# A hybrid encoder block whose input projection begins with a block of 512 tokens, taken slice by slice of the features

## The chip, the cores and the metric

The kernel runs on one core of a Trainium2 chip. A core has a matrix engine (TensorE, PE in the profile, with PEld for its weight loads), VectorE (DVE), ScalarE (ACT), GpSimd (POOL) and SyncE (SP), which here issues the transfers. The metric is the device time of one execution in microseconds (us); the median of several executions is compared.

## The reference

One layer of an encoder over 2048 tokens of 1024 features, all in float32. What matters here is its head:

```python
xn = rms_norm(h, ln_mix_g[l])          # x / sqrt(mean(x*x) + eps) * g
proj = xn @ w_in[l]                    # 1024 x 2512 columns
y_a = mlstm_group(proj[..., OFF_Q:OFF_K], proj[..., OFF_K:OFF_V], proj[..., OFF_V:OFF_O],
                  proj[..., OFF_O:OFF_G], proj[..., OFF_G:OFF_CQ] + b_gates[l], ...)
y_b = mla_group(proj[..., OFF_CQ:OFF_CKV], proj[..., OFF_CKV:OFF_KR], proj[..., OFF_KR:IN_COLS], ...)
h = h + concatenate([y_a, y_b]) @ w_out[l]
```

The last 464 columns of the projection, called the rest here, are 16 gates, a query latent of 256, a key/value latent of 128 and 64 columns that are rotated by position. Behind the mixer come a gated feed-forward with a convolution, a gated per-layer embedding and a final norm.

## The kernel before

Every float32 operand of a projection is split in a high part, rounded to the type of TensorE's fast path, and a low part, the remainder. A product is three matmuls: low x high, high x low, high x high. `split` makes the high part of x with a ScalarE copy and the low part with a VectorE subtraction; `split_g` does the same for weights and multiplies them by the norm's gain (`gcol`) on the way. The factor 1/rms of a token is applied behind the matmul, from `rcol`, one column for each tile of 128 tokens.

`in_proj` (line 176) runs four stages over the 16 token tiles (`st`): the rest columns, the v columns, the o columns, and the q and k columns.

- *The rest stage.* `load_w` fetches the 464 columns of weights in pairs of feature slices of 128 and splits them into eight tiles. `load_x` fetches one token tile of x, all 1024 features of 128 tokens, 512 KB. In step `st` of the loop tile `st + 1` is loaded, tile `st` is split, the norm of tile `st - 1` is summed (`ssq_x`), the projection of tile `st - 2` is done (`rest`, which calls `nat`: 24 matmuls of 464 columns into one PSUM bank) and a tile two steps older is transposed (`turn_rest`). The first tile comes in two halves between the first weight slices (`first`).
- *The norm.* `ssq_x` squares x on ScalarE, adds on VectorE, sums over the partitions with small matmuls against `ones` into a tile of the pool `ml`, which has a single buffer, and takes the power -1/2 on GpSimd. VectorE reads the sum out of PSUM in line 239 (214 in the changed kernel).
- *What `rest` does behind its matmuls.* It writes the gates to `gt`, scales the other columns out of PSUM (`rs`), norms the two latents, rotates 64 columns and leaves the result in `nn`; `turn_rest` transposes that on TensorE and stores it.
- *The v and o stages.* Each tile is 24 matmuls of 512 columns; the output goes through a buffer taken from the rotation `trot` (tags t0 to t3 in turn) and is stored. Behind the first tiles of the v stage stand the last `turn_rest` calls, and from tile 2 on one step per tile of `gates`, a generator that prepares the gate values.
- *The q and k stage.* Its convolution (`taps`, `silu`) takes its tiles from the same `trot`. The last three, for `j` = 7, are made in `tail`, beside the first tiles of attention: there `other`, the mLSTM's generator, runs its first seven steps, one buffer of `trot` is skipped, three `taps` follow, and some steps later three Silu, pinned to their order. The mLSTM's `load_v` puts chunk c of v into the tag t0 or t1 (`c % 2`), from chunk 15 downwards, and its running state starts in t2.
- *PSUM.* The pool `sc` has four banks (`bank`), `tr` two (`tbank`), `pv` one, `ml` one.

The order of the instructions on each engine comes from a planner, except inside `manual_schedule`, where the listed engines keep the order of the code. It is fixed when the program is built. SP issues nearly all transfers, in one queue; a transfer that waits for a buffer holds up those behind it. Buffers are named by tags: a new tile with a tag waits until the readers of the old one are done. The tags w9 to w12 (`rrot`) hold in turn the raw weights and the token tiles of x; w13 holds the squares.

Of the kernel before, what the change touches and what calls it, by code (L numbers as in the profile page):

```python
# [19 lines left out]
P = 128  # L20
S = 2048
D = 1024
KT = D // P
NT = S // P
# [5 lines left out]
OFF_R = 2048  # L30
NREST = W_IN_COLS - OFF_R
# [2 lines left out]
PLE = 256  # L34
EPS = 1e-6
SB = 512
LAG_T, LAG_X, LAG_R = 1, 2, 2
SIDE = 668
KSCALE = 128.0 ** -0.5
ASCALE = 192.0 ** -0.5  # L40
# [12 lines left out]
def _rot(kind, idx):  # L53
    idx = list(idx)
    i = 0
    while True:
        yield f"{kind}{idx[i % len(idx)]}"
        i += 1


class Block:
# [114 lines left out]
    def in_proj(self):  # L176
        nc, d = self.nc, self.d
        xh = [[self.at(f"x{4 * c + 2 * f}", [P, 4, 512], F32R, f"xh{c}{f}") for f in range(2)] for c in range(4)]
        xl = [[self.at(f"x{4 * c + 2 * f + 1}", [P, 4, 512], F32R, f"xl{c}{f}") for f in range(2)] for c in range(4)]
        wrot, rrot, trot, srot = _rot("w", (*range(9), 13)), _rot("w", range(9, 13)), _rot("t", range(4)), _rot("s", range(3))  # L180
        w_in = d["w_in"][0].rearrange("(a b p) c -> a p b c", b=2, p=P)

        def load_w(c0, n, before=None):

            out, raws = [], []

            def load(k2, parts=1):
                raw = self.at(next(rrot), [P, 2, 512], name="wraw")
                for i in range(parts):
                    bs = slice(2 * i // parts, 2 * (i + 1) // parts)  # L190
                    nc.sync.dma_start(raw[:, bs, :n], w_in[k2, :, bs, c0:c0 + n])
                raws.append(raw)
                return raw

            if before:
                load(0, 2)
                before(0)
                load(1, 2)
                before(1)
                load(2)  # L200
                load(3)
            for k2 in range(KT // 2):
                if k2 == len(raws):
                    load(k2)
                raw = raws[k2]
                for b in range(2):
                    w = self.at(next(wrot), [P, 2, 512], F32R, "wsp")
                    self.split_g(raw[:, b, :n], gcol[:, 2 * k2 + b:2 * k2 + b + 1], w[:, 0, :n], w[:, 1, :n])
                    out.append(w)
            return out  # L210

        def nat(st, ws, n):
            ps = self.bank()
            c, o = st // 4, (st % 4) * P
            for kt in range(KT):
                f, k = divmod(kt, 4)
                self.mm3(ps[:, :n], xh[c][f][:, k, o:o + P], xl[c][f][:, k, o:o + P],
                         ws[kt][:, 0, :n], ws[kt][:, 1, :n], kt == 0, kt == KT - 1)
            return ps

        def load_x(st):

            t = self.at(next(rrot) if st else "u2", [P, KT, P], name="x_t")
            if st:
                nc.sync.dma_start(t, d["x_turned"][:, :, st * P:(st + 1) * P])
            return t

        def ssq_x(st, x_t):

            sq = self.at("w13", [P, KT, P], name="x_sq")  # L230
            nc.scalar.activation(sq, x_t, AF.Square)
# [3 lines left out]
            ps = self.pml.tile([P, 4], F32, name="ssp", tag="ml")  # L235
            for i in range(2):
                nc.tensor.matmul(ps, ss[:, i], ones, start=i == 0, stop=i == 1)
            t = self.stat(1, "rsm")
            nc.vector.tensor_scalar(t, ps[:, 0:1], 1.0 / D, EPS, op0=ALU.mult, op1=ALU.add)
            nc.gpsimd.tensor_tensor(rcol[:, st:st + 1], t, self.nhalf[:, :1], op=ALU.pow)  # L240
# [7 lines left out]
        def rest(st):  # L248
            ps = nat(st, ws, NREST)
# [28 lines left out]
        def turn_rest(st, nn):  # L278
            pt = self.ppv.tile([P, 4, P], F32, name="rtp", tag="pv")
            for j in range(4):  # L280
                nc.tensor.transpose(pt[:, j, :], nn[:, j * P:(j + 1) * P], self.ident)
# [5 lines left out]
        nc.sync.dma_start(gcol, d["g_turned"])  # L287
        rcol = self.cst.tile([P, NT], F32, name="rcol")
        ones = self.cst.tile([P, 4], F32, name="ones")
        nc.vector.memset(ones, 1.0)  # L290
        nq, xq = {}, {}

        xq[0] = load_x(0)

        def first(f):

            fs = slice(4 * f, 4 * f + 4)
            if f < 2:
                nc.sync.dma_start(xq[0][:, fs], d["x_turned"][:, fs, 0:P])
# [1744 lines left out]
```

## Time and profile before

| what | us |
|---|---|
| median of 3 executions | 2901.97 |
| lowest, highest | 2898.76, 2902.77 |
| the profiled execution's own time | 2898.51 |
| its span, first to last instruction | 2896.7 |
| TensorE busy | 2854.7 |
| VectorE, ScalarE busy | 2029.8, 1524.2 |

The page gives for each engine the busy time, then groups of instructions by line. In a row of the timeline the first number is the start in the span, the second the length, then engine, line, operation, output and inputs, and how often; in brackets stands the idle time before it and what ended it. SPq rows are transfers being issued. In a table of windows each row is a stretch of time with the busy time of PE, PEld, DVE, ACT and POOL, the granted TensorE clock (1.00 is full), the DMA share and GB/s. TensorE is the engine that is nearly always busy, so what counts is where it is idle or slow.

### The profile page before, as it was taken

To read this page: it belongs to the slowest core of one execution; us is meant where nothing else is said; L and a number is where in the kernel's file an instruction comes from. 1 tells how busy PE (TensorE), PEld (TensorE's weight loads), DVE (VectorE), ACT (ScalarE), POOL (GpSimd) and SP (SyncE) were. 2 spreads that over 40 slices of the span, in tenths; PEclk is the share of its full clock that TensorE was granted. 3 is DMA by queue.
4 is the path that set the end of the run, shared out by engine and by line. 5 is a ranking of instruction groups with operands and counts; after the bars stand their busy time and mean duration, and the time that the engine had idled before them with its cause. 6 is when DMAs were issued, how large, how long until landed. Compare 5 with 4: busy or idle time off the path is not lost.

```text
span 2896.7 us, 41145 instructions
## 1 busy us (share of the span) xinstructions
PE 2854.7 (99%) x14622; PEld 2416.9 (83%) x14622; DVE 2029.8 (70%) x3758; ACT 1524.2 (53%) x3014; POOL 157.1 (5%) x295
## 2 busy tenths in 40 slices
PE   8999999999999999999999999999999999999998
PEld 7888888888888889888788888888888788888787
DVE  7521555777777777776777877867777867676787
ACT  7311544556666666665755555655556333254665
POOL 3100000000000010001000000000000000011111
PEclk9999999999999999999999999999999999999999
DMA  6512545653332333378844554657766757576764
GB/s 189 132 59 77 162 125 163 218 162 117 105 111 98 97 104 113 126 244 267 276 145 165 193 174 147 220 176 235 234 230 210 241 187 249 166 265 205 263 217 163
DMA packets 408318, 509.00 MB, mean 176 GB/s; under 512 B 34080, under 2 KB 271664, under 8 KB 408112
## 3 DMA queue, kind: packets, MB, share of 16 engines
q1 hardware_dynamic: 408112, 506.37, 53.8%
q8 instruction: 115, 1.88, 0.3%
q14 instruction: 91, 0.75, 0.1%
HBM read 324.16 MB, written 182.12 MB: 175 GB/s over the span
## 4 chain that ended last, share of the span: by engine, by line
PE 58%; DMA 3%; DVE 3%; issue 2%; ACT 2%; POOL 0%; POOLq 0%; SPq 0%; ACTq 0%; DVEq 0%
PE fy L1434 21%; PE fz L1434 14%; PE fx L1434 14%; PE ppv L133 2%; PE fs L133 1%; PE tb L977 1%; DMA opr<-t_d 1%; DMA h_d<-xt 1%; PE bk L914 1%; PE bk L916 1%; PE bk L915 1%; PE bk L917 1%; PE bk L918 1%; DMA opr<-tw_d 1%; DVE op L123 1%
## 5 line engine op out<-in xcount | busy, mean ns | idle before, releaser
L1434 PE MATMUL fz<-op,fw 128*128 128x512 f32 x1968 | 478.8, 391 | 4.5 <-ACT fw L120 4.0
L1434 PE MATMUL fx<-op,fw 128*128 128x512 f32 x1968 | 476.4, 390 | 0.0
L1434 PE MATMUL fy<-op,fw 128*128 128x512 f32 x1968 | 475.3, 390 | 0.6 <-ACT fy L1546 0.6
L1434 PEld LDWEIGHTS fz<-op,fw 128*128 128x128 f32 x1968 | 368.4, 188 | 82.4 <-ACT fw L120 5.4
L1434 PEld LDWEIGHTS fy<-op,fw 128*128 128x128 f32 x1968 | 368.6, 188 | 77.3 <-ACT fy L1546 1.0
L1434 PEld LDWEIGHTS fx<-op,fw 128*128 128x128 f32 x1968 | 368.2, 188 | 76.1 <-ACT fy L1546 0.2
L1434 PE MATMUL fy<-op,fwd 128*128 128x512 f32 (+1 forms) x984 | 238.2, 390 | 1.9 <-DVE uv L1419 1.5
L120 ACT CAST pt<-tb 128x512 fp32r<-128x512 f32 x256 | 147.3, 587 | 172.1 <-PE tb L977 171.5
L133 PE MATMUL bk<-wsp,xh 128*128 128x512 f32 (+1 forms) x768 | 234.3, 386 | 0.0
L919 DVE TENSOR_REDUCE mx<-bk 128x1 f32<-128x512 f32 x256 | 174.8, 684 | 59.8 <-PE bk L918 58.8
L1434 PEld LDWEIGHTS fy<-op,fwd 128*128 128x128 f32 x984 | 182.6, 188 | 40.6 <-DVE uv L1419 2.6
L133 PE MATMUL ppv<-pt,kv 128*128 128x256 f32 x1536 | 205.2, 287 | 0.4 <-DVE pt L123 0.3
L123 DVE TENSOR_TENSOR pt<-tb,pt 128x512 fp32r<-128x512 f32 x256 | 173.9, 683 | 31.4 <-ACT pt L120 29.2
L937 ACT ACTIVATE pe<-bk,nm 128x512 f32<-128x512 f32 x256 | 174.8, 695 | 37.8 <-DVE nm L931 33.0
L133 PEld LDWEIGHTS ppv<-pt,kv 128*128 128x128 f32 x1536 | 189.3, 191 | 0.9 <-DVE pt L123 0.5
L133 PEld LDWEIGHTS bk<-wsp,xh 128*128 128x128 f32 x768 | 145.3, 189 | 25.0
L133 PE MATMUL bk<-wsp,xl 128*128 128x512 f32 (+1 forms) x384 | 150.6, 392 | 7.4 <-DVE xl L123 7.4
L133 PE MATMUL bk<-xh,wqk 128*128 128x512 f32 x480 | 157.1, 393 | 0.0
L977 PE MATMUL tb<-ident,pe 128*128 128x128 f32 x1024 | 151.0, 273 | 3.8 <-DVE pt L123 3.7
L977 PEld LDWEIGHTS tb<-ident,pe 128*128 128x128 f32 x1024 | 121.7, 140 | 23.4 <-DVE pt L123 6.0
L120 ACT CAST fw<-hraw 128x1024 fp32r<-128x1024 f32 (+1 forms) x72 | 70.2, 980 | 115.7 <-PE fx L1434 58.7
L120 ACT CAST op<-opr 128x512 fp32r<-128x512 f32 x165 | 95.9, 621 | 58.3 <-DMA opr<-tw_d 17.6
(360 smaller groups left out, 4915.3 us busy)
## 6 DMA issues: line engine op xcount, KB each, us to landing
fwr<-in_w_up SPq DMA_DIRECT2D x66, 512.0 KB, 5.2
fh<-h_d SPq DMA_DIRECT2D x48, 512.0 KB, 4.3
h_d<-fh SPq DMA_DIRECT2D x48, 512.0 KB, 4.1
s_d<-fwr SPq DMA_DIRECT2D x44, 512.0 KB, 3.2
fws<-s_d SPq DMA_DIRECT2D x44, 512.0 KB, 3.5
rw<-row_d SPq DMA_DIRECT2D x32, 512.0 KB, 5.1
tw_d<-tsum SPq DMA_DIRECT2D x60, 256.0 KB, 5.3
opr<-tw_d SPq DMA_DIRECT2D x60, 256.0 KB, 5.1
```

Of the source, the lines that this page charges most:

```text
L120: nc.scalar.copy(hi, src)
L123: (sub or nc.vector).tensor_tensor(lo, src, _f(hi), op=ALU.subtract)
L133: mm = lambda *a, **k: self.nc.tensor.matmul(*a, **k, skip_group_check=more)
L914: mm(ps, ql, kh[:, ks], start=True, stop=False)
L915: mm(ps, qr, self.krl[:, ks], start=False, stop=False)
L916: mm(ps, qh, kl[:, ks], start=False, stop=False)
L917: mm(ps, qr, self.kr2[:, ks], start=False, stop=False)
L918: mm(ps, qh, kh[:, ks], start=False, stop=True)
L919: nc.vector.tensor_reduce(s.mx[:, kb:kb + 1], ps, axis=AX.X, op=ALU.max)
L937: nc.scalar.activation(s.pe[:, kb % 2], s.banks[kb], AF.Exp, bias=s.nm, scale=ASCALE, accum_out=s.rs[:, kb:kb + 1])
L977: nc.tensor.transpose(t[:, j, :], s.p[kb][:, j * P:(j + 1) * P], self.ident)
L1434: nc.tensor.matmul(out, a[:, k * P:(k + 1) * P], parts[lo][:, cols], start=first, stop=lo == 1 and k == last, skip_group_check=more)
```

## The change

It touches the rest stage alone, and the places where the v stage takes over.

- The first four token tiles are one block (`first_block`). x comes in eight slices of 128 features by 512 tokens (256 KB, tags t0 to t7) instead of by token tiles; slice and weights alternate on SP's queue, and the gain vector moves to ScalarE's queue. For each slice twelve matmuls run, four tiles each of high x high, low x high and high x low, into the four banks of `sc`.
- The squares of the block are taken from the slices on ScalarE and added up on VectorE in one tile `acc`; the norm of each of its four tiles is then one small matmul on a quarter of `acc` (`inv_rms`).
- A one-element ScalarE copy (`warm`) stands at the head, and eight matmuls of the identity matrix with itself. Head and block are under `manual_schedule` for TensorE, VectorE and ScalarE.
- Tiles 4 and 5 use the two banks of `tr`; from tile 6 on the banks of `sc` come round. The work behind the matmuls (`rest`) runs three tiles late (`finish`), so five turns, not two, are left to the v stage, and `gates` starts there at tile 5 instead of 2.
- `trot` becomes t6, t7, and then t0, t1, t3, t2 in turn.

```diff
-        wrot, rrot, trot, srot = _rot("w", (*range(9), 13)), _rot("w", range(9, 13)), _rot("t", range(4)), _rot("s", range(3))
+        wrot, rrot, trot, srot = _rot("w", (*range(9), 13)), _rot("w", range(9, 13)), chain(("t6", "t7"), _rot("t", (0, 1, 3, 2))), _rot("s", range(3))
...
-        def nat(st, ws, n):
-            ps = self.bank()
+        def nat(st, ws, n, ps=None):
+            ps = self.bank() if ps is None else ps
...
+            t = xq[st] = self.at(next(rrot), [P, KT, P], name="x_t")
+            nc.sync.dma_start(t, d["x_turned"][:, :, st * P:(st + 1) * P])
+
+        def inv_rms(st, parts):
+
+            ps = self.pml.tile([P, 4], F32, name="ssp", tag="ml")
+            for i, p in enumerate(parts):
+                nc.tensor.matmul(ps, p, ones, start=i == 0, stop=i == len(parts) - 1)
+            t = self.stat(1, "rsm")
+            nc.vector.tensor_scalar(t, ps[:, 0:1], 1.0 / D, EPS, op0=ALU.mult, op1=ALU.add)
+            nc.gpsimd.tensor_tensor(rcol[:, st:st + 1], t, self.nhalf[:, :1], op=ALU.pow)
...
+            inv_rms(st, (ss[:, 0], ss[:, 1]))
...
+        def first_block():
+
+            raws, xr = [], []
+            for kt in range(KT):
+                if kt % 2 == 0:
+                    raws.append(self.at(next(rrot), [P, 2, 512], name="wraw"))
+                xr.append(self.at(f"t{kt}", [P, 512], name="x_c"))
+                if kt < 2:
+                    nc.sync.dma_start(raws[0][:, kt, :NREST], w_in[0, :, kt, OFF_R:OFF_R + NREST])
+                    if kt == 0:
+                        nc.scalar.dma_start(gcol, d["g_turned"])
+                elif kt % 2 == 0:
+                    nc.sync.dma_start(raws[kt // 2][:, :, :NREST], w_in[kt // 2, :, :, OFF_R:OFF_R + NREST])
+                nc.sync.dma_start(xr[kt], d["x_turned"][:, kt, 0:512])
+            ps = [self.bank() for _ in range(4)]
+            acc = self.at("u2", [P, 512], name="x_a")
+            for kt in range(KT):
+                f, k = divmod(kt, 4)
+                w = self.at(next(wrot), [P, 2, 512], F32R, "wsp")
+                self.split_g(raws[kt // 2][:, kt % 2, :NREST], gcol[:, kt:kt + 1], w[:, 0, :NREST], w[:, 1, :NREST])
+                self.split(xr[kt], xh[0][f][:, k, :], xl[0][f][:, k, :])
+                ws.append(w)
+                for n, (x, e) in enumerate(((xh, 0), (xl, 0), (xh, 1))):
+                    for st in range(4):
+                        nc.tensor.matmul(ps[st][:, :NREST], x[0][f][:, k, st * P:(st + 1) * P], w[:, e, :NREST],
+                                         start=kt == 0 and n == 0, stop=kt == KT - 1 and n == 2)
+                if kt:
+                    sq = self.at(f"u{kt % 2}", [P, 512], name="x_q")
+                    nc.scalar.activation(sq, xr[kt], AF.Square)
+                    nc.vector.tensor_tensor(acc, acc, sq, op=ALU.add)
+                else:
+                    nc.scalar.activation(acc, xr[0], AF.Square)
+            return ps, acc
+
+        def rest(st, ps):
...
-        nq, xq = {}, {}
-
-        xq[0] = load_x(0)
-
-        def first(f):
-
-            fs = slice(4 * f, 4 * f + 4)
-            if f < 2:
-                nc.sync.dma_start(xq[0][:, fs], d["x_turned"][:, fs, 0:P])
-                self.split(xq[0][:, fs], xh[0][f][:, :, 0:P], xl[0][f][:, :, 0:P])
-
-        ws = load_w(OFF_R, NREST, first)
-        for st in range(NT + LAG_X):
-            if st + 1 < NT:
-                xq[st + 1] = load_x(st + 1)
-            if st == 0:
-                gn = self.at("t5", [P, 384], name="gn")
-                self.row_bcast(gn[:, 0:256], d["q_norm_g"][0], 256)
-                self.row_bcast(gn[:, 256:384], d["kv_norm_g"][0], 128)
-                bg = self.row_bcast(self.cst.tile([P, 16], F32, name="bg"), d["b_gates"][0], 16)
-            if 1 <= st < NT:
-                split_x(st, xq[st])
-            if 0 <= st - 1 < NT:
-                ssq_x(st - 1, xq.pop(st - 1))
-            if 0 <= st - LAG_X < NT:
-                nq[st - LAG_X] = rest(st - LAG_X)
-            if 0 <= st - LAG_X - LAG_R < NT:
-                turn_rest(st - LAG_X - LAG_R, nq.pop(st - LAG_X - LAG_R))
+        warm = self.stat(1, "warm")
+        nc.scalar.activation(warm, self.nhalf[:, 0:1], AF.Copy, scale=2.0)
+        wp = self.pml.tile([P, P], F32, name="warm", tag="ml")
+        nq, xq, done, ws = {}, {}, {}, []
+        ET = mybir.EngineType
+
+        def finish(st):
+            if 0 <= st < NT:
+                nq[st] = rest(st, done.pop(st))
+            if 0 <= st - LAG_R < NT:
+                turn_rest(st - LAG_R, nq.pop(st - LAG_R))
+
+        with self.tc.manual_schedule(engines={ET.PE, ET.DVE, ET.Activation}):
+            for _ in range(8):
+                nc.tensor.matmul(wp, self.ident, self.ident, start=True, stop=True)
+            ps, acc = first_block()
+        done.update(enumerate(ps))
+        for st in (4, 5):
+            load_x(st)
+        gn = self.at("t5", [P, 384], name="gn")
+        self.row_bcast(gn[:, 0:256], d["q_norm_g"][0], 256)
+        self.row_bcast(gn[:, 256:384], d["kv_norm_g"][0], 128)
+        bg = self.row_bcast(self.cst.tile([P, 16], F32, name="bg"), d["b_gates"][0], 16)
+        for st in (4, 5):
+            split_x(st, xq[st])
+        for st in range(4):
+            inv_rms(st, (acc[:, st * P:(st + 1) * P],))
+        for st in range(4, NT):
+            if st + 2 < NT:
+                load_x(st + 2)
+            done[st] = nat(st, ws, NREST, self.tbank([P, 512]) if st < 6 else None)
+            ssq_x(st, xq.pop(st))
+            if st + 2 < NT:
+                split_x(st + 2, xq[st + 2])
+            for i in ((0, 1), (2,), (3,), (4,), (5,))[st - 4] if st < 9 else (st - 3,):
+                finish(i)
...
-            if st < LAG_R:
-                turn_rest(NT - LAG_R + st, nq.pop(NT - LAG_R + st))
+            if st < 5:
+                finish(NT - 3 + st)
-            if st >= LAG_R:
+            if st >= 5:
```

More of the change, by code (lines that the diff above doesn't have):

```diff
@@ L36 @@
 SB = 512
-LAG_T, LAG_X, LAG_R = 1, 2, 2
+LAG_T, LAG_R = 1, 2
 SIDE = 668
@@ L179, in in_proj, with load_w @@
         xl = [[self.at(f"x{4 * c + 2 * f + 1}", [P, 4, 512], F32R, f"xl{c}{f}") for f in range(2)] for c in range(4)]
-        wrot, rrot, trot, srot = _rot("w", (*range(9), 13)), _rot("w", range(9, 13)), _rot("t", range(4)), _rot("s", range(3))
+        wrot, rrot, trot, srot = _rot("w", (*range(9), 13)), _rot("w", range(9, 13)), chain(("t6", "t7"), _rot("t", (0, 1, 3, 2))), _rot("s", range(3))
         w_in = d["w_in"][0].rearrange("(a b p) c -> a p b c", b=2, p=P)
-        def load_w(c0, n, before=None):
-            out, raws = [], []
-            def load(k2, parts=1):
+        def load_w(c0, n):
+            out = []
+            for k2 in range(KT // 2):
                 raw = self.at(next(rrot), [P, 2, 512], name="wraw")
[L189 to L205, printed above, removed]
+                nc.sync.dma_start(raw[:, :, :n], w_in[k2, :, :, c0:c0 + n])
                 for b in range(2):
@@ L221, in load_x @@
         def load_x(st):
[L223 to L226, printed above, removed]
+            t = xq[st] = self.at(next(rrot), [P, KT, P], name="x_t")
[7 more added lines that the diff above has]
+            nc.gpsimd.tensor_tensor(rcol[:, st:st + 1], t, self.nhalf[:, :1], op=ALU.pow)
         def ssq_x(st, x_t):
@@ L234, in ssq_x @@
             nc.vector.tensor_tensor(ss[:, 0:2], ss[:, 0:2], ss[:, 2:4], op=ALU.add)
[L235 to L240, printed above, removed]
+            inv_rms(st, (ss[:, 0], ss[:, 1]))
         def split_x(st, x_t):
@@ L245, in split_x @@
                 self.split(x_t[:, 4 * f:4 * f + 4], xh[c][f][:, :, o:o + P], xl[c][f][:, :, o:o + P])
-        def rest(st):
-            ps = nat(st, ws, NREST)
+        def first_block():
[31 more added lines that the diff above has]
+        def rest(st, ps):
             rx = rcol[:, st:st + 1]
@@ L286, in in_proj @@
         gcol = self.cst.tile([P, KT], F32, name="gcol")
-        nc.sync.dma_start(gcol, d["g_turned"])
         rcol = self.cst.tile([P, NT], F32, name="rcol")
```

## Prediction

> **What bounds the kernel now.** I read the page first, then the timeline of the first 125 us, then the places where TensorE waits later on.
>
> ```profile
> PE 2854.7 (99%) x14622; PEld 2416.9 (83%) x14622; DVE 2029.8 (70%) x3758; ACT 1524.2 (53%) x3014; POOL 157.1 (5%) x295
> ```
>
> TensorE is busy 2854.7 of 2896.7 us: all its idle time is 42 us. A change at the head of the program can win the head's idle and slow stretches, and every wait it adds on TensorE counts in full, for the stages behind run in order.
>
> ```profile
> 0.72 0.40 SPq L287 DMA_DIRECT2D gcol<-in_g_turned  x1
> 1.18 0.89 SPq L191 DMA_DIRECT2D wraw<-in_w_in  x2
> 4.03 1.28 ACT L128 ACT_TABLE_LOAD   x1 [4.03 <-DMA wraw<-in_w_in]
> 5.33 0.68 ACT L128 ACTIVATE wsp<-wraw,gcol 128x464 fp32r<-128x464 f32 x1
> 5.99 0.62 ACT L120 CAST xh<-x_t 128x512 fp32r<-128x512 f32 x1
> 7.40 0.75 PE L133 MATMUL bk<-wsp,xl 128*128 128x464 f32 x1 [7.40 <-DVE xl L123]
> 8.72 0.59 PE L133 MATMUL bk<-wsp,xl 128*128 128x464 f32 x1
> 9.88 0.59 PE L133 MATMUL bk<-wsp,xl 128*128 128x464 f32 x1
> ...
> 12.77 0.37 PE L133 MATMUL bk<-wsp,xl 128*128 128x464 f32 x1
> 13.39 0.38 PE L133 MATMUL bk<-wsp,xl 128*128 128x464 f32 x1
> ...
> 59.50 0.60 PE L281 MATMUL rtp<-ident,nn 128*128 128x128 f32 x4
> 65.40 0.60 PE L281 MATMUL rtp<-ident,nn 128*128 128x128 f32 x4
> ...
> 106.63 0.48 PE L133 MATMUL bk<-wsp,xl 128*128 128x512 f32 x1
> 118.09 0.60 PE L281 MATMUL rtp<-ident,nn 128*128 128x128 f32 x4
> 118.44 0.47 PE L133 MATMUL bk<-wsp,xl 128*128 128x512 f32 x1
> ```
>
> Three things are to be seen. TensorE starts at 7.40, behind transfer, table load, two casts and a subtraction. Its first matmuls go at half speed: three in 1.16 us (8.72 to 9.88, 0.387 each), later three in 0.62 (0.208 each). From then a token tile takes 5.90 us (59.50 to 65.40): 24 matmuls, one norm sum, one turn. The v stage begins at 106.63; a turn in it holds TensorE for 0.35 (118.09 to 118.44), 0.4 with the slow restart behind it.
>
> **The change part by part.** *First matmul.* The first weight slice is issued at 0.72 instead of 1.18. It took 4.03 - 1.18 = 2.85 us, so it lands at 3.57. The table load now runs ahead, in `warm`; the gain vector goes out on ScalarE's queue. The x slice is issued second, at about 1.17.
>
> ```profile
> x_t<-in_x_turned SPq DMA_DIRECT2D x1, 256.0 KB, 3.9
> 10.00:20.00 10.00, 9.57 (x44) 7.89 (x43) 8.74 (x20) 8.36 (x13) 1.65 (x2) 1.00 1.02 285
> 10.52 2.39 ACT L128 ACTIVATE wsp<-wraw,gcol 128x464 fp32r<-128x464 f32 x4
> 11.26 2.53 DVE L129 SCALAR_TENSOR_TENSOR wsp<-wraw,gcol,wsp 128x464 fp32r<-128x464 f32 x4
> 13.84 1.29 DVE L123 TENSOR_TENSOR xl<-x_t,xh 128x512 fp32r<-128x512 f32 x2
> 15.70 1.14 ACT L120 CAST xh<-x_t 128x512 fp32r<-128x512 f32 x2 [0.41 <-DMA x_t<-in_x_turned]
> 14.23 1.05 ACT L231 ACTIVATE x_sq<-x_t 128x1024 f32<-128x1024 f32 x1
> ```
>
> A slice of that size took 3.9 us behind two weight slices (row one); behind one it is bounded by 2.85 and 3.9. I take 3.3: it lands at 4.5, is cast by 5.1, and TensorE, which now wants only the high halves, starts at 5.2 (4.7 to 5.8) instead of 7.40.
>
> *The block of 512 tokens.* 96 matmuls of 0.208 are 20.0 us, to 25.2; if the eight warm-up matmuls achieve nothing, the first twelve cost 0.18 more each, and it ends at 27.3. Each slice asks 2.5 us of TensorE. ScalarE needs 0.60 + 0.57 + half of 1.05 = 1.7, VectorE 0.63 + 0.64 + 0.64 = 1.9, and 488 KB at 285 GB/s (second row) are 1.7. So all three hide; VectorE ends at 4.3 + 8 x 1.91 = 19.6. On SP's queue the q-norm gain has to wait until slice 5's buffer is free, about 15.5, and holds tile 6's load behind it to about 17; with 4.2 us of landing (below) it comes before ScalarE wants it at about 22. This hides.
>
> *The norm sums, the new wait.* In the changed program TensorE's order after the block is the norm sum of tile 0, two matmuls of tile 4, the norm sum of tile 1, and so on. All four use the one bank of pool `ml`, so the second waits until VectorE has read the first (line 214). In VectorE's order that read stands behind the low halves of tiles 4 to 9, and tile 9's load needs tile 5's buffer, which ScalarE's square frees, which waits for a sum on VectorE.
>
> ```profile
> DMA to landing us min/median/max: 3.7/4.2/5.5
> L240 POOL TENSOR_TENSOR rcol<-rsm,nhalf 128x1 f32<-128x1 f32 x16 | 14.8, 925 | 42.3 <-DVE rsm L239 42.3
> ```
>
> These are the landing of the x tiles and the power on GpSimd. Chain: 19.6 + four halves 2.6 + tile 4's sum 0.64 = 22.8; square of tile 5 1.05 to 23.9; load of tile 9 4.2 to 28.1; two casts 1.14 and a low half 0.65 to 29.9; the read 0.15: 30.1 (29.6 to 31.4 by 3.7 and 5.5). TensorE is there at 26.0 (28.1 unwarmed) and stands 4.1 (2.0) us. So the warm clock is worth nothing here. The next two sums each wait for power and two short steps, about 1.3, against 0.8 of matmuls: the fourth sum goes at 32.7. Eighteen matmuls of tile 4 end at 36.8, its sum at 37.2, tile 5 at 42.3; ten tiles of 5.90 and a last sum and turn: the v stage begins at 102.2, 4.4 early. It holds five turns instead of two: 3 x 0.4 = 1.2. Banks do not wait: tile 6 is due at 43, tile 0's bank is read by about 33.
>
> *Half clock after the stall.* A long wait in this trace shows what follows one:
>
> ```profile
> 2717.71 1.21 PE L1434 MATMUL fz<-op,fw 128*128 128x512 f32 x4 [2.71 <-ACT fw L120]
> 2718.00:2719.00 1.00, 1.00 (x5) 0.67 (x5) 1.00 (x2) 0.66 (x2) 1.00 (x1) 0.92 1.04 289
> 2721.00:2722.00 1.00, 1.00 (x4) 0.81 (x3) 0.40 (x2) 0.94 (x1) 0.00 (x0) 0.50 1.10 387
> 2722.00:2724.00 2.00, 2.00 (x9) 1.60 (x9) 2.00 (x3) 0.59 (x1) 0.00 (x0) 0.94 0.98 385
> ```
>
> The third number from the right is the granted clock. After 2.71 idle microseconds it stood at 0.50 from 2718.8 (0.92 in the slice) to 2722.2 (0.94 in two), 3.4 us from about 1.1 after the restart. The same here loses half of that, 1.6, less what the next two waits swallow: 0.8 (0 to 1.6). By the Trainium skill's "TensorE: Matmul & The Clock Gate" (table "Why this matters for your kernels") only gaps over about 3 us drop the clock; the rows show 2.71 doing it. By the page the 4.1 would drop the clock and the 2.0 of an unwarmed block would not, and the head would be 0.8 better there.
>
> Head in all: -4.4 + 1.2 + 0.8 = -2.4 (-4 to 0).
>
> *Far behind: the start of attention.* The output buffers now rotate as t6, t7, then 0, 1, 3, 2. After 61 uses and one skipped, the last three convolution tiles get t0, t1, t3 instead of t2, t3, t0, and t1 is held by v of chunk 15 (`load_v`). So one tap waits for TensorE, and in ScalarE's order the three Silu stand in two groups instead of one, with two more table loads, ahead of an Exp.
>
> ```profile
> 522.58 0.59 ACT L120 CAST pt<-tb 128x512 fp32r<-128x512 f32 x1 [1.02 <-PE tb L977]
> 523.19 1.28 ACT L414 ACT_TABLE_LOAD   x1
> 524.37 3.11 PE L133 MATMUL ppv<-pt,kv 128*128 128x256 f32 x24
> 524.48 1.67 ACT L414 ACTIVATE ct<-ct 128x512 f32<-128x512 f32 x3
> 526.27 1.28 ACT L937 ACT_TABLE_LOAD   x1
> 528.40 0.50 PE L914 MATMUL bk<-kv,q_s 128*128 128x512 f32 x1 [0.47 <-ACT pe L937]
> 558.44 0.71 PE L767 MATMUL mb<-v,kk 128*128 128x129 f32 x4 [0.96 <-DVE kk L760]
> 580.95 0.71 PE L767 MATMUL mb<-v,kk 128*128 128x129 f32 x4 [1.08 <-DVE cb L771]
> ```
>
> Now the group starts 1.2 us before the 24 value matmuls that cover it and TensorE waits 0.47. The first new group has one Silu, is 1.1 us shorter, and that 0.47 goes. The second stands behind the last cast of its tile and a tap, so it starts about 0.7 after its cover does: 1.9 later, one Silu (0.56) shorter, 0.4 for the tap: 0.47 + 1.9 - 0.56 + 0.4 = 2.2 (0 to 2.8). Two loads also make ScalarE 2.6 us later for the chunk loop, whose order runs through VectorE; I let its two waits of 0.96 and 1.08 come once more: 2.0 (0 to 5). Together -0.5 + 2.2 + 2.0 = +3.7 (-0.5 to +7.3). By the Trainium skill's "ScalarE: Activation LUTs" (What ACT_TABLE_LOAD costs) a switch costs about 2.66 us with its drain, so two would be 5.3; the trace has the Silu 0.01 us after the 1.28, so I stay with 2.6.
>
> *Sum.* -2.4 + 3.7 = +1.3. The profiled execution took 2898.51, 1.8 of it around the span of 2896.7, so it would take 2899.8. It lies 3.46 under the median of the runs, 2901.97; for the median I say 2903.3.
>
> **The rivals.** *The rotation costs nothing* (for it: the first group now costs 0.47 with a table pair in it; against: the second starts later). Then the head counts and the 0.47: -2.9, 2899.1.
>
> *The rotation costs more, and the kernel is slower.* Place: TensorE's waits on ScalarE and VectorE between 510 and 620 us. If VectorE falls behind the chunk loop there, each later chunk waits, 5 us instead of 2, and the wait of 2.2 is followed by half clock, 1.6: -0.5 + 2.2 + 5.0 + 1.6 = 8.3 on a head at its poor end, 0: 2910.3. It decides where the added waits come to 6 us more than the head wins.
>
> *The new wait is not there, and the kernel is faster.* If the second norm sum did not stand for VectorE's read, the 4.1 and two times 0.5 would go too, with the half clock: the head would win 3.2 + 5.1 = 8.3: 2897.4 with the rotation's price, 2893.7 without. Against it stands the order of both engines, which is fixed before the run.
>
> **How the numbers follow.** The forecast has 0.46, the free rotation 0.25, the dear one 0.21, the missing wait 0.08. The range holds the head's -4 with a free rotation (2898) and reaches to the dear one (2910). A measurement of this kernel, whose runs spread over 4 us, can hardly tell less than 0.2% (5.8 us) from nothing. Below 2896.2 lies the last case with a cheap rotation: 0.06. Above 2907.8 lies the dear case, less a little: 0.20. Within: 0.74.
>
> **What would show it.** The first matmul of the block near 5.2; TensorE idle 2 to 4 us near 26 to 30 before a norm sum, put down to VectorE, and half clock behind it; the v stage near 102; two Silu groups and a TensorE wait of about 2 us near 540. I am wrong if the norm sums do not wait, if the warm clock decides the block, or if the waits between 510 and 620 grow by under 1 or over 7 us.

## The result, and the profile after

| | before | changed |
|---|---|---|
| median, us | 2901.81 (6 executions) | 2912.24 (6 executions) |
| lowest, highest | 2898.76, 2905.19 | 2907.04, 2917.44 |
| ratio, 95% interval | | 1.0035, 1.0024 to 1.0045 |
| profiled execution: time, span | 2898.51, 2896.7 | 2913.11, 2911.3 |

The change makes the kernel 10.4 us slower. The forecast, 2903.3 with a range to 2910, was wrong: the kernel lies 2.2 us above the range. Where the time went is read from the start of the first matmul with the same operands in the two timelines:

| first matmul of | before | changed | difference |
|---|---|---|---|
| the v stage | 106.63 | 103.79 | -2.84 |
| the q and k stage (`bk<-xh,wqk`) | 283.33 | 287.11 | +3.78 |
| attention's scores (`bk<-kv,q_s`) | 493.77 | 497.91 | +4.14 |
| `mb<-qk` in the mLSTM | 667.07 | 680.65 | +13.58 |
| the feed-forward stage (`fx<-op,fw`) | 1234.07 | 1246.61 | +12.54 |
| end of the span | 2896.7 | 2911.3 | +14.6 |

So there are two losses: 6.6 us in the v and o stages, from -2.84 to +3.78, and 9.4 us in the first part of attention, from +4.14 to +13.58. The head wins 2.8.

The head of the changed kernel in its timeline:

```profile
4.89 1.38 PE L256 MATMUL bk<-wsp,xh 128*128 128x464 f32 x4
25.42 0.28 PE L212 MATMUL ssp<-ones,x_a 128*128 128x4 f32 x2
29.11 1.14 ACT L120 CAST xh<-x_t 128x512 fp32r<-128x512 f32 x2 [1.36 <-DMA x_t<-in_x_turned]
31.18 0.59 PE L212 MATMUL ssp<-ones,x_a 128*128 128x4 f32 x2 [4.96 <-DVE rsm L214]
103.79 0.48 PE L133 MATMUL bk<-wsp,xl 128*128 128x512 f32 x1
```

And in windows:

```profile
29.00:30.00 1.00, 0.00 (x0) 0.00 (x0) 0.24 (x1) 0.89 (x2) 0.00 (x0) 0.69 0.00 0
30.00:35.00 5.00, 3.82 (x13) 3.48 (x14) 3.11 (x18) 2.46 (x9) 2.19 (x5) 0.50 0.00 0
36.00:37.00 1.00, 1.00 (x5) 0.86 (x5) 0.64 (x2) 0.00 (x0) 0.83 (x4) 0.89 0.16 36
```

The block runs as forecast, from 4.89 to 25.42. Then the second norm sum waits 4.96 us for VectorE to read the first. That read comes behind the last low halves, and these come behind a tile of x that lands late. The clock is 0.50 from 29.4, still in the wait, to 36.2 (0.69 and 0.89 are the shares of the first and the last microsecond): 6.8 us.

The v stage of the changed kernel in its timeline: transfers as they are issued (SPq), ScalarE, TensorE.

```profile
106.14 0.37 SPq L344 DMA_DIRECT2D r_d<-rcol  x1
111.96 5.33 SPq L301 DMA_DIRECT2D rest_d<-rt  x1
123.06 0.33 SPq L147 DMA_DIRECT2D go<-in_mlstm_norm_g  x1
125.57 0.56 SPq L549 DMA_DIRECT2D ukvt<-in_w_ukv_turned  x1
129.53 0.50 ACT L120 CAST uvs<-ukvt 128x128 fp32r<-128x128 f32 x2 [12.33 <-DMA ukvt<-in_w_ukv_turned]
129.94 0.58 ACT L300 COPY rt<-rtp 128x512 f32<-128x512 f32 x1
130.57 0.66 PE L298 MATMUL rtp<-ident,nn 128*128 128x128 f32 x4 [3.27 <-ACT rt L300]
```

Its transfers by group between 104 and 125 us (KB each, median us from issue to landing), and a window behind the wait:

```profile
rest_d<-rt SPq DMA_DIRECT2D x3, 256.0 KB, 3.6
r_d<-rcol SPq DMA_DIRECT2D x1, 8.0 KB, 12.1
```

```profile
130.00:135.00 5.00, 4.43 (x15) 3.62 (x16) 1.15 (x4) 1.10 (x3) 0.00 (x0) 0.68 0.52 157
```

This wait was not forecast. The 8 KB of `r_d<-rcol` (1/rms, 2048 pieces of 4 bytes) take 12.1 us to land, and transfers behind them take up to 5.33 us to issue instead of 0.52. The gain row `go` of the o stage has to wait until the first v output has left tag t6, and holds up the transfer behind it, `ukvt`, a weight that attention needs. In ScalarE's order the casts of `ukvt` stand ahead of the copy of a turn out of PSUM. Turns have only one bank there, so TensorE waits 3.27 us before the next turn, with half clock behind it.

The start of attention: first a window of the kernel before; then, of the changed kernel, rows of ScalarE and the longest waits of TensorE but one (1.78 us, the same in both kernels); then its windows:

```profile
500.00:660.00 160.00, 154.39 (x1006) 136.75 (x1005) 120.09 (x293) 91.09 (x210) 1.42 (x2) 1.00 0.59 187
```

```profile
527.29 1.28 ACT L438 ACT_TABLE_LOAD   x1
528.58 0.63 ACT L438 ACTIVATE ct<-ct 128x512 f32<-128x512 f32 x1
541.84 1.15 ACT L438 ACTIVATE ct<-ct 128x512 f32<-128x512 f32 x2 [0.37 <-DVE ct L433]
545.14 0.79 PE L938 MATMUL bk<-kv,q_s 128*128 128x512 f32 x1 [2.58 <-ACT pe L961]
565.22 1.09 PE L779 MATMUL mb<-ident,kTb 128*128 128x128 f32 x4 [2.54 <-DVE cb L795]
581.39 0.71 PE L791 MATMUL mb<-v,kk 128*128 128x129 f32 x4 [1.71 <-DVE kk L784]
```

```profile
546.00:548.00 2.00, 2.00 (x6) 1.52 (x6) 1.93 (x5) 1.86 (x6) 0.00 (x0) 0.50 1.06 339
566.00:568.00 2.00, 2.00 (x9) 1.81 (x8) 1.84 (x5) 1.17 (x2) 0.00 (x0) 0.50 0.78 252
584.00:586.00 2.00, 2.00 (x12) 2.00 (x11) 1.34 (x6) 1.52 (x4) 0.00 (x0) 0.56 0.76 209
500.00:660.00 160.00, 150.35 (x942) 132.20 (x941) 114.39 (x272) 87.20 (x192) 0.00 (x0) 0.97 0.55 170
```

The three Silu now stand in two groups, one and two. In this window TensorE is idle 160 - 150.35 = 9.65 us against 5.61 before, and each of the three waits has half clock behind it, where before there was none. The window ends before the changed kernel has done the same work. Counted from the first score to `mb<-qk`, with 1084 matmul records in both traces, TensorE is idle 10.71 us against 5.61 and busy 172.03 against 167.69: of the 9.4 us, 5.1 are waiting, and in the other 4.3 the same matmuls take longer.

### The profile page after: what moved, and what is told of

The parts are those of the page before. It is cut to its first block, busy times and chain, and to the rows that moved or that the text cites. A ratio compares the mean times of both kernels' runs of the same rounds, so it can differ in the third digit from the quotient of the medians.

```text
span 2911.3 us, 41169 instructions
## 1 busy us (share of the span) xinstructions
PE 2863.1 (98%) x14630; PEld 2424.3 (83%) x14630; DVE 2031.6 (70%) x3757; ACT 1526.1 (52%) x3021; POOL 151.7 (5%) x295
## 4 chain that ended last, share of the span: by engine, by line
PE 79%; DMA 5%; DVE 5%; ACT 3%; issue 3%; POOL 0%; SPq 0%; POOLq 0%; ACTq 0%; DVEq 0%
PE fy L1458 20%; PE fz L1458 13%; PE fx L1458 13%; PE bk L133 11%; PE ppv L133 5%; PE tb L1001 3%; PE bk L938 2%; PE bk L940 2%; PE bk L941 2%; PE bk L939 2%; PE bk L942 2%; PE fs L133 1%; PE gb L133 1%; DMA h_d<-xt 1%; PE mb L876 1%
## 5 line engine op out<-in xcount | busy, mean ns | idle before, releaser
L133 PE MATMUL bk<-wsp,xh 128*128 128x512 f32 (+1 forms) x672 | 205.7, 387 | 0.0
L133 PEld LDWEIGHTS bk<-wsp,xh 128*128 128x128 f32 x672 | 127.0, 189 | 23.6
L133 PE MATMUL bk<-wsp,xl 128*128 128x512 f32 (+1 forms) x336 | 132.2, 394 | 0.0
```

Of the source, the lines that this page charges most:

```text
L133: mm = lambda *a, **k: self.nc.tensor.matmul(*a, **k, skip_group_check=more)
```

## The experiments

Times are medians, each with its ratio to the kernel before from the same series and its 95% interval. Differences to the changed kernel are between medians of different series, in which the kernel before itself had 2900.8 to 2902.5.

**rot: the tags of the q and k stage as before.**

```diff
         urot, wrot = _rot("u", (0, 1, 2)), _rot("w", (6, 9, 10, 11))
+        trot = _rot("t", range(4))
```

> The changed kernel, but at the q and k stage the output buffers start again as t0, t1, t2, t3, as in the kernel before, so that the last three taps get t2, t3, t0. Nothing else differs. Theory (the tags alone cost the start of attention): the three Silu stand in one group again, TensorE's waits between 510 and 620 fall from about 9 to about 3 us, none is followed by half clock, and the 9.4 us that the changed kernel loses between its first score matmul (497.9) and 667 shrink to under 1. Time 2912.2 - 9 = about 2903, ratio to before 1.0005. Rival (attention starts in another phase against its transfers, whatever the tags): waits of 2.5 us stay there, and the time stays above 2908. The v stage keeps its wait of 3.3 us in both.

Measured: 2907.23, ratio 1.0013 (1.0005 to 1.0022), 5.0 under the changed kernel. The same stretch in its windows:

```profile
500.00:660.00 160.00, 154.46 (x998) 136.66 (x997) 120.98 (x290) 91.43 (x209) 1.41 (x2) 1.00 0.58 183
```

Idle time and clock are those of the kernel before again; from the first score (498.14, +4.37) to `mb<-qk` (671.25, +4.18) nothing is lost, where the changed kernel lost 9.4. The place and the mechanism are as the theory said; the medians moved by 5.0 and not 9. Five of its eleven executions took 2902.57 to 2904.26, six took 2907.23 to 2910.17. The profiled one (2903.29) is of the five, so it doesn't show what the other six lost.

**before_rot: the same tags, put into the kernel before.**

```diff
         urot, wrot = _rot("u", (0, 1, 2)), _rot("w", (6, 9, 10, 11))
+        trot = _rot("t", (3, 2, 0, 1))
```

> The kernel before, with one line more: at the q and k stage its output buffers go round as t3, t2, t0, t1, which gives the last three taps t0, t1, t3, as in the changed kernel; head and v stage stay. Theory (these tags alone split the three Silu in two groups and make attention start late): the first score matmul stays at 493.8, waits of about 2.5 us come at 540 and 560, 5 to 9 us are lost by 667, and the time is 2907 to 2911, ratio 1.0015 to 1.003. Rival (they cost only in the phase that the changed head gives): under 2 us lost by 667, time within 2902 to 2905.

Measured: 2910.72, ratio 1.0026 (1.0016 to 1.0036), 8.2 slower than the kernel before. One line, far from the head, costs 8.2 where the whole change costs 10.4. In its timeline, and in windows:

```profile
542.52 0.50 PE L915 MATMUL bk<-kv,q_s 128*128 128x512 f32 x1 [2.58 <-ACT pe L938]
562.10 1.07 PE L756 MATMUL mb<-ident,kTb 128*128 128x128 f32 x4 [2.10 <-DVE cb L772]
```

```profile
544.00:546.00 2.00, 1.99 (x10) 1.51 (x11) 1.97 (x5) 1.38 (x5) 0.00 (x0) 1.00 1.03 359
564.00:566.00 2.00, 2.00 (x8) 1.52 (x7) 1.21 (x2) 0.59 (x2) 0.00 (x0) 0.60 0.85 216
```

The waits stand where those of the changed kernel stand: 2.58, 2.10 and 1.40 us instead of 2.58, 2.54 and 1.71, here with half clock behind the second alone. The distance to the kernel before grows from 1.56 at the first score to 10.58 at `mb<-qk`; of these 9.0 us, 6.1 are more idle time of TensorE (11.73 against 5.61). (The first score came at 495.33, not 493.8; this profile had 1.6 us more before it.)

All profiles agree on the place. From the first score to `mb<-qk`, the seven with the tags t0, t1, t3 (changed, `before_rot`, and below `store`, `go`, `sums`, `head`, `nowarm`) lose 6.5 to 10.0 us against the first profile of the kernel before; the six with t2, t3, t0 (`rot`, and below `all3`, `best`, `best_cold`, `cold3`, `before2`) lose -0.2 to 1.9.

**store: 1/rms transposed, then stored in 16 pieces.**

```diff
-        nc.sync.dma_start(self.r_d.rearrange("(t p) -> p t", p=P), rcol)
+        rp = self.tbank([NT, P], name="rcp")
+        nc.tensor.transpose(rp, rcol, self.ident)
+        rw = self.at(next(srot), [NT, P], name="rcw")
+        nc.vector.tensor_copy(rw, rp)
+        nc.sync.dma_start(self.r_d.rearrange("(t p) -> t p", p=P), rw)
```

> The changed kernel, but the sixteen columns of 1/rms are transposed on TensorE and stored as 16 pieces of 512 bytes instead of 2048 pieces of 4 bytes. The order of transfers and of ScalarE stays. Theory (the store of 4-byte pieces holds the queue for some 12 us, so the gain row of the o stage, then a weight load, then ScalarE's casts of it, then the copy of a turn come late): the wait of 3.3 us at a turn near 130 and the half clock behind it go, 4.9 us together, for 0.3 us of transposing: 2907.5, ratio 1.0018; the gain row is issued before 116 instead of at 123. Rival 1 (the gain row shares tag t6 with the first v output and would be late anyhow): a wait of 2 us or more stays at a turn, and the time stays near 2911. Rival 2 (five turns are too many for one bank): the same. The start of attention is as in the changed kernel.

Measured: 2910.42, ratio 1.0026 (1.0017 to 1.0035), 1.8 under the changed kernel, which the intervals don't tell from nothing. In its timeline:

```profile
105.51 0.28 PE L345 MATMUL rcp<-ident,rcol 128*16 128x128 f32 x1 [1.66 <-POOL rcol L215]
112.05 0.52 SPq L301 DMA_DIRECT2D rest_d<-rt  x1
115.15 0.42 SPq L147 DMA_DIRECT2D go<-in_mlstm_norm_g  x1
121.05 0.42 SPq L553 DMA_DIRECT2D ukvt<-in_w_ukv_turned  x1
```

The queue flows again, `go` goes out at 115.15 instead of 123.06, and no turn waits. The transpose brought a wait of its own, 1.66 us for the last power on GpSimd, because the planner put it too far forward. The q and k stage begins at 283.31, 3.8 us earlier than in the changed kernel. The first part of attention still loses 6.5 us. Why only 1.8 of the 3.8 arrives in the median is not shown.

**go: the gain row gets a tag for itself; the 4-byte store stays.**

```diff
-chain(("t6", "t7"), _rot("t", (0, 1, 3, 2)))
+chain(("t7",), _rot("t", (0, 1, 3, 2)))
...
+        trot = _rot("t", (3, 2, 0, 1))
         ws = load_w(OFF_O, 512)
```

> The changed kernel, but the first v output takes t7 instead of t6, the others t0, t1, t3, t2 in turn as before from the o stage on, so that the gain row of the o stage has t6 for itself and is issued early, as in the kernel before. The store of 4-byte pieces stays where it is. Theory A (the 4-byte store is enough to hold the queue): the store of a turn still takes some 5 us to issue and the wait at the turn stays at 2 us or more. Theory B (it takes both, the store and the gain row that waits for the first v output to land): the wait at the turn falls under 1 us, and the first score matmul comes 4 to 5 us earlier than in the changed kernel (497.9).

Measured in one execution: 2904.47. Theory B holds in its trace. The store of a turn behind the 4-byte pieces still took 4.58 us to issue, but `ukvt` no longer waits for the gain row:

```profile
111.84 4.58 SPq L301 DMA_DIRECT2D rest_d<-rt  x1
120.48 0.45 SPq L550 DMA_DIRECT2D ukvt<-in_w_ukv_turned  x1
```

`ukvt` is issued 5 us earlier, and the wait at the turn is under 0.6. The first score comes at 492.79 instead of 497.91. So the wait took both parts: the 4-byte store, which the kernel before has too, and the gain row that the new rotation put behind the first v output. Taking either away is enough.

**sums: the four norm sums in four parts of one bank.**

```diff
+        ps4 = self.pml.tile([P, 4, 4], F32, name="ssp", tag="ml")
         for st in range(4):
-            inv_rms(st, (acc[:, st * P:(st + 1) * P],))
+            nc.tensor.matmul(ps4[:, st], acc[:, st * P:(st + 1) * P], ones, start=True, stop=True)
+        t4 = self.stat(4, "rsm")
+        nc.vector.tensor_scalar(t4, ps4[:, :, 0], 1.0 / D, EPS, op0=ALU.mult, op1=ALU.add)
+        nc.gpsimd.tensor_tensor(rcol[:, 0:4], t4, self.nhalf[:, :4], op=ALU.pow)
```

> The changed kernel, but the four norm sums of the block go into four parts of one bank, with one read on VectorE and one power on GpSimd for all four, so that no sum waits for the read of the one before. Theory (the wait of 4.96 us is the bank of the sums alone, and half clock follows it): both go, 4.96 + 1.6 = 6.6 us; the v stage begins near 97.2 instead of 103.8; time 2905.7, ratio 1.0012. Rival (VectorE is late with everything there, so the wait only moves to a low half or to a norm sum of a token tile): a wait of 2 us or more stays between 25 and 45, and the v stage begins after 101.

Measured: 2912.39, ratio 1.0037 (1.0023 to 1.0051): no change. My theory fell, and the rival was right. In its timeline:

```profile
31.14 0.16 DVE L336 TENSOR_SCALAR rsm<-ssp 128x4 f32<-128x4 f32 x1
41.55 0.42 DVE L223 TENSOR_TENSOR x_ss<-x_ss 128x256 f32<-128x256 f32 x1
42.12 0.98 PE L212 MATMUL ssp<-ones,x_ss 128*128 128x4 f32 x4 [4.73 <-DVE x_ss L223]
103.99 0.48 PE L133 MATMUL bk<-wsp,xl 128*128 128x512 f32 x1
```

The sums go through at once, TensorE works on to 37.4, and then waits 4.73 us for the norm sum of tile 5: VectorE reads the block's sums at 31.14, no earlier than in the changed kernel (30.98), and in its order the squares of tile 5 stand behind most of the work of the block's four tiles, which waits for that read. The bank was only where the lateness showed.

**all3: rot, store and sums together.**

> The three edits together: buffers of the q and k stage as before, the 1/rms stored in 16 pieces, the four norm sums in one bank. Theory (the three losses are separate and add): 2912.2 - 9.4 - 4.6 - 6.6 = 2891.6, ratio to before 0.9965. Rival (what is won at the head is given back at waits farther on, in attention or the feed-forward stage): over 2896, ratio over 0.998, with new waits behind 600.

Measured: 2899.96, ratio 0.9991 (0.9982 to 1.0000), 8.4 above the theory, which had counted 6.6 for a wait that only moves (`sums`) and nothing for the wait of the transpose. The number is on the rival's side (over 2896), but the rival's new waits are not there: between 600 and 1460 us each wait of TensorE over 1 us stands at an instruction where one stands in the second profile of the kernel before (`before2`, below).

**head: the order written out by hand on to tile 4.** The four sums as in `sums`; the loads of tiles 4 and 5 and their split in high and low parts move into the block's written-out order, and the sums with the first step of the loop (`step`, the loop's body as a function) get a section like it.

```diff
             ps, acc = first_block()
+            for st in (4, 5):
+                load_x(st)
+                split_x(st, xq[st])
...
+        with self.tc.manual_schedule(engines={ET.PE, ET.DVE, ET.Activation}):
...
+            for st in range(4, 5):
+                step(st)
+        for st in range(5, NT):
+            step(st)
```

> The changed kernel with the four norm sums in one bank, as in the run sums, and the order of TensorE, VectorE and ScalarE written out by hand on to token tile 4, so that VectorE reads the sums behind the low halves of tiles 4 to 6 or 7 instead of 4 to 9 and takes the squares of tile 5 ahead of most of the work of the block's four tiles. Theory (the head is set by VectorE's order: the read stands behind low halves whose loads are late, and all later work of the tiles behind the read): the wait of 4.7 to 5.0 us is gone at both places, what is left are waits under 1.5 us without half clock, the v stage begins between 98 and 100 instead of 103.8, and the time is 4 to 6 us under that of the changed kernel, about 2907. Rival (the transfers set it: the tiles of x come no faster): the v stage begins at 103 or later, wherever the wait lies, and the time stays at 2912.

Measured: 2908.37, ratio 1.0021 (1.0012 to 1.0030), 3.9 under the changed kernel. The v stage begins 4.1 us earlier:

```profile
28.47 0.15 DVE L346 TENSOR_SCALAR rsm<-ssp 128x4 f32<-128x4 f32 x1
35.68 0.42 DVE L223 TENSOR_TENSOR x_ss<-x_ss 128x256 f32<-128x256 f32 x1
99.70 0.48 PE L133 MATMUL bk<-wsp,xl 128*128 128x512 f32 x1
```

The read comes 2.7 us and the squares of tile 5 5.9 us earlier than in `sums`, and the waits that are left in the head are under 1 us. The loads of tiles 6 and 7 were issued no earlier (17.80 and 19.61, in `sums` 17.31 and 19.13). VectorE's order set the head, not the transfers.

**nowarm: without the matmuls on the identity.**

```diff
-            for _ in range(8):
-                nc.tensor.matmul(wp, self.ident, self.ident, start=True, stop=True)
```

> The changed kernel without the eight matmuls on the identity. Theory (TensorE waits for the read of the norm sums anyhow, so a warm clock in the block wins nothing): the block's first matmuls go at half speed and it ends near 27.3 instead of 25.4, the wait for the second norm sum shrinks from 4.96 to about 3.1, the v stage begins at 103.3 to 104.3 as before this edit, and the time is that of the changed kernel, 2912, ratio 1.0035. Rival (the clock decides the head): the v stage begins at 105.5 or later and the time is 2 us longer.

Measured: 2906.80, ratio 1.0012 (1.0003 to 1.0022): 5.4 faster than with them. Neither theory had that.

```profile
5.06 1.91 PE L256 MATMUL bk<-wsp,xh 128*128 128x464 f32 x4 [5.06 <-ACT xh L120]
28.37 0.15 DVE L214 TENSOR_SCALAR rsm<-ssp 128x1 f32<-128x1 f32 x1
98.60 0.48 PE L133 MATMUL bk<-wsp,xl 128*128 128x512 f32 x1
```

The block's first matmuls go at half speed (four in 1.91 us against 1.38) and it ends 2.35 us later (27.77), 0.17 of it a later start. But the v stage begins 5.2 us earlier. With the eight matmuls away the planner gave VectorE another order: the first read stands behind nine low halves of token tiles, in the changed kernel behind twelve. Behind the block TensorE has no idle time left up to 100 us. So this run changes the clock and the order together; the next two keep the order.

**best and best_cold: the clock without a change of order.** `best` is `head` with the tags of `rot` and the transposed store, which here stands behind the fourth v tile; `best_cold` is that without the eight matmuls, with the order of the engines the same but for one low half.

> The run head with the two other edits: buffers of the q and k stage as before, and the 1/rms transposed and stored in 16 pieces, here behind the fourth tile of the v stage, so that TensorE does not wait for the last power. Theory (the three losses are separate): all3 took 2900.0; the head gives 4 to 5 and the transpose 1.7 more, so 2894, ratio to before 0.997. Rival (what the head wins is given back at waits farther on): 2898 or more, ratio over 0.9985.

> The run best without the eight matmuls on the identity; the order of all engines stays, but for one low half on VectorE. This parts the clock from the order, which changed together in nowarm. Theory (VectorE sets the head; TensorE, 2.3 us later out of the block, waits that much less, of which best has 1.6 to 2 us near 39 and half clock behind it): the v stage begins at 99.0 to 100.3 as in best (99.6), the time stays within 2 us of 2895. Rival (the clock counts now that the long wait is gone): v stage at 101.5 or later, time 2897 or more.

Measured: `best` 2895.05, ratio 0.9975 (0.9966 to 0.9984); `best_cold` 2894.63, ratio 0.9978 (0.9970 to 0.9987). The v stage begins at 99.59 and at 100.00. The two ratios differ by 0.0003, well inside their intervals: the warm clock is worth nothing that these runs can tell, as forecast, even without the long wait. What the three edits win arrives at the end: `best` reaches `mb<-qk` 18.1 us earlier than the changed kernel, and its median is 17.2 lower.

**cold3: nowarm with the tags of rot and the transposed store of best.**

> The run nowarm with two more edits: buffers of the q and k stage as before, and the 1/rms stored in 16 pieces behind the fourth tile of the v stage. In nowarm the planner itself put VectorE's reads of the norm sums further forward, no wait was left in the head, and the v stage began at 98.6 although the block ended 2.3 us later. Theory (order of VectorE, tags and store are the three losses, the clock of the block is not one): v stage near 98.6, the wait of 3.1 us at a turn gone, waits of 2.5 us at 540 and 560 gone, time 2906.8 - 8 - 4.6 = 2894, the same as the run best within 3 us. Rival (the warm clock is worth its 2.3 us): 2897 or more.

Measured: 2891.87, ratio 0.9969 (0.9957 to 0.9982), 9.0 under the kernel before. Its v stage begins at 97.93. A row of its timeline and two windows show that the losses are gone: the three Silu stand in one group, no wait is left behind the block, and the start of attention is as in the kernel before:

```profile
517.42 1.68 ACT L442 ACTIVATE ct<-ct 128x512 f32<-128x512 f32 x3
```

```profile
30.00:35.00 5.00, 5.00 (x29) 4.56 (x28) 3.69 (x23) 2.82 (x12) 4.60 (x9) 1.00 0.10 26
500.00:660.00 160.00, 153.63 (x1021) 136.89 (x1020) 121.53 (x294) 92.20 (x215) 1.41 (x2) 1.00 0.60 188
```

This is the block of 512 tokens without its three losses, and it is faster than both kernels.

**before2: a second profile of the kernel before.**

> The kernel before, unchanged, for a second profile. Its purpose: all changed profiles but one lose 2 to 4 us between 1310 and 1440, where the order of the instructions is that of the kernel before. Theory (those waits hang on where the transfers happen to stand, and differ from execution to execution): the second profile shows a wait of 2 to 3 us near 1383, where the first has 1.00, or other waits that differ by 1 us and more. Rival (the changes cause them): the second profile repeats the first within 0.3 us at each wait.

Measured: 2904.98, against 2898.51 of the first profile.

```profile
1386.84 1.12 PE L1715 MATMUL fs<-ident,xt 128*128 128x128 f32 x4 [2.49 <-ACT nt_o L1717]
1434.24 1.05 PE L1715 MATMUL fs<-ident,xt 128*128 128x128 f32 x4 [2.14 <-ACT xt L1705]
```

The first profile had 1.00 us at the first of these places (1383.22). The second program is the same, and it loses 5 us more between 1309 and 1440. So the last steps of the table above, from +13.58 to +12.54 and to +14.6, are within what differs between executions, and can't be put down to the change.

## Why the prediction was wrong, point by point

- *First matmul at 5.2, block to 25.2.* Right: 4.89 and 25.42.
- *The second norm sum at 30.1, a wait of 4.1.* Right in place, cause and size: the read came at 30.98 (the range said 29.6 to 31.4), the sum at 31.18, the wait was 4.96. The half clock was mis-sized: two times 3.4 us instead of one, and begun within the wait. From the restart at 31.18 to 36.2 it costs half of 5.0, less what the next two waits swallow, where 0.8 was said. The v stage came at 103.79 instead of 102.2 + 0.8.
- *"If the second norm sum did not stand for VectorE's read, ... the head would win 8.3."* Wrong as a rival's price: `sums` took that wait away and won nothing, since everything behind the read on VectorE is late as well. `head` and `nowarm` show what wins: an earlier read.
- *"So the warm clock is worth nothing here."* Right as far as the runs can tell (`best_cold`). What the step did not see is that the eight matmuls also move the planner's order of VectorE, at 5 us (`nowarm`).
- *"It holds five turns instead of two: 3 x 0.4 = 1.2."* **This step failed.** The v and o stages lost 6.6: 1.2 for the turns, 3.27 for the wait at a turn, and half of 3.4 us of half clock, 1.7. I counted the turns on TensorE and did not follow them through ScalarE's copy and SP's queue. The trace of before had it. There the gain row was fetched early, and the same store of 4-byte pieces was issued at 96.69:

```profile
27.34 0.43 SPq L147 DMA_DIRECT2D go<-in_mlstm_norm_g  x1
96.69 0.38 SPq L320 DMA_DIRECT2D r_d<-rcol  x1
```

  The stores of turns behind it, in the group of transfers between 95 and 115 us, show how slow the queue then was:

```profile
rest_d<-rt SPq DMA_DIRECT2D x3, 256.0 KB, 11.0
```

  That is 11.0 us to landing, where 2.6 is the least of the 16 stores and 3.9 their median. Before, two turns stood in that place; the change put five there, and the gain row behind the first v output. By the Trainium skill's "DMA: Bandwidth & Descriptors" (Bandwidth) transfers under 64 KB are ruled by their descriptors, not their bytes; the 8 KB that took 12.1 us agree.
- *The start of attention, "+3.7 (-0.5 to +7.3)".* **This term was mis-sized.** It cost 9.4 in the trace. The waits were forecast in the right places: the one on the first group is gone, the second is 2.58 (2.2 said), and all idle time from the first score to `mb<-qk` grew by 5.1 (3.7 said). What I left out is half clock behind these waits, though the paragraph on the head had shown that such a wait can have it: three stretches of 3.4 us, in which the matmuls took 4.3 us longer. How much of the loss is clock differs between profiles with these tags: `sums` had no half clock there, 5.7 us more idle time, and lost 6.8.
- *The rival with the dear rotation, 2910.3,* had the place and the sign, and its number is 1.9 from the median. In part that is luck: it had 5.0 in the chunk loop, where about 3 came, one stretch of half clock, where three came, and a head worth 0, where head, v and o stages together cost 3.8.
- *The rivals' free rotation* is excluded by `before_rot`: 8.2 us for the tags alone.
- *The sum.* +1.3 was said for the profiled execution and +14.6 came. The 13.3 that were missing: 0.8 at the head, 5.4 in the v and o stages, 0.4 up to attention, 5.7 in its first part, 1.0 behind it, where executions differ by more than that.

Open is the share of each loss in the medians: `rot` took back 5.0 and `before_rot` cost 8.2 for the same tags, `store` took back 1.8 for 3.8 us in the trace. Executions of one kernel spread over 4 to 11 us, and a profile shows one of them. What a profile wins at 283 may be lost at a wait farther on; no run here shows where.

## What to carry to other kernels

Follow an added step along every queue that it crosses, not only on the engine that bounds the kernel: the five late turns were cheap on TensorE and dear on SP and ScalarE. When a wait goes, ask which later instruction of the same engine was late with it; only an earlier read moved the head, not a second bank. Price a wait of about 2 us or more on TensorE with slow clock behind it as the likely case (in the first 700 us of the fourteen profiles, 13 of the 19 waits of 2.1 to 3.8 us had it), and check the order of all engines after an edit that seems to be local: a rotation of tags chosen for the head split an activation group 400 us later, and eight idle matmuls reordered VectorE.

## What the runs showed of the hardware that I had not expected

The length of a wait alone does not tell whether half clock follows, where it is below 4 us. In `best`, in its timeline and in a window:

```profile
512.55 0.50 PE L953 MATMUL bk<-kv,q_s 128*128 128x512 f32 x1 [1.79 <-ACT pe L976]
```

```profile
515.00:516.00 1.00, 1.00 (x4) 0.60 (x4) 0.00 (x0) 0.00 (x0) 0.00 (x0) 0.50 0.64 102
```

After 1.79 us the clock is 0.50. In `cold3` the same instruction waits as long (510.86), and the clock stays at 1.00; so it does after the 2.58 us in `before_rot` (542.52, its rows stand above) and after the 3.17 us before a turn in `sums` (130.68). After the 4.96 us of the changed kernel it is 0.50 for 6.8 us, and not for 3.4; the five other waits of 4.6 us or more behind the block (`rot`, `store`, `go`, `sums`, `all3`) have 6.8 too. The Trainium skill's "TensorE: Matmul & The Clock Gate" (Part 1, What's actually happening) says that activity is judged in windows of some 3.4 us that run freely, and that the clock falls after at least one idle window. Free windows agree with equal waits that end differently, and 6.8 is twice the window; but 1.79 us of idling is less than the page asks for, and here the measurement decides.

A store of 8 KB in pieces of 4 bytes took 12.1 us to land, where the stores of 256 KB in pieces of 512 bytes took 3.9 in the median and 2.6 at best in the kernel before. A transfer behind it took up to 5.33 us to issue; with the 8 KB in pieces of 512 bytes (`store`) the same transfer took 0.52.
